# First weight differences on VectorE, the exponential's table behind the last split, and fewer clock-keeping products in a two-layer decoder trunk

## The chip, the core and the metric

The kernel runs on one core of a Trainium2 chip. The metric is the device time of one execution in microseconds; before the change it is 1159.97 us, the median of three runs (1159.62 to 1160.34). The engines are named as in the profile: PE is TensorE (matrix products), PEld its weight loads, DVE is VectorE, ACT is ScalarE, POOL is GpSimd and SP is SyncE, which issues DMAs. Each engine runs its own queue in order, and waits on semaphores of the others.

## The reference

256 tokens of 1024 values pass through two layers. Each layer projects the token matrix once, for three mixers: latent attention with a rotary key, a gated delta rule and a gated recurrence (HGRN2). It merges them by gates and adds a mixture of experts (one of four groups, two of its eight experts).

```
c_q, c_kv, k_rope, qkv, beta, a, ... = split(x @ w_in)          # one combined projection
cos, sin = rope_tables(positions)
o_mla = mla_branch(c_q, c_kv, k_rope, ...)
g = -exp(a_log) * softplus(a + dt_bias)                          # decay of the delta rule
o_dn  = gated_deltanet_branch(qkv, beta, a, ...)
o_hg  = hgrn2(...)
x = LN(alpha*x + mix(o_mla, o_dn, o_hg));  x = LN(alpha*x + moe(x))
```

## The kernel before, in words

The projection needs the normalised tokens with their channels on the partitions. So each layer starts with a norm (`centred` and `norm_scale`: L354 on ScalarE subtracts the mean, L327 to L344 on VectorE work out the scale `rs`, in steps on tiles of 128x2). At L619 VectorE makes two diagonal matrices of `rs`, the tile `sg`. `transposed` multiplies the tokens with them on TensorE (L395, 32 products in two parts, `pm` and `pb`), so that one product turns and scales. ScalarE (L401) and VectorE (L403) evict the results with the norm's gain and bias.

All large products work on split operands: a value is kept as a coarse part and the difference to it, `hTh` and `hTl` for the tokens (L254 on ScalarE, L255 on VectorE, four of each per layer), `wh` and `wl` for weights. `split` makes the latter per piece of 128x1024: a cast on ScalarE (L249) and the difference at L250, on VectorE, or on GpSimd where the piece's name stands in the set `POOLED` (L143). `mm3` then does three products per pair (L261 to L263). The first weights of a layer are those of `cq` (the attention's query rank), in two pieces, `cq.0` and `cq.1`; both names stand in `POOLED`.

Behind `cq` comes `dn_decay`: 24 products with 72 columns (the rotary key and the gates' logits, whose small weights are split at L689 and L691), then a step that loads ScalarE's table with exponential and logarithm (L696), and the decay's own steps (L699 to L752), with the exponential of `a_log` at L719. Then `mla` begins with `ckv` and the sums of squares (L1169 to L1174), and further on `dn_keys` with its first weight `dn_k0`. In layer 0 only, `rope_tables` (L432 to L464) makes sine and cosine from the positions, a chain of VectorE steps on 128x256 tiles with ScalarE's sine (L454, L455) in it; the step at L702 needs them.

What sets the order: a scheduler places each engine's instructions by its own estimates of when operands are ready; `issue_after(x)` keeps what is inside it behind instruction x; SyncE's transfers go in the order of their issue.

The clock-keeping products are `warm(n)`: n products of a constant tile, whose result nobody reads. There are 12 at the start, 8 in layer 0 behind the transposing products (inside `layer`) and 14 between the layers (L1718), in front of the norm.

Of the kernel before, what the change touches and what calls it, by code (L numbers as in the profile page):

```python
# [14 lines left out]
AF = mybir.ActivationFunctionType  # L15
OP = mybir.AluOpType
# [3 lines left out]
DEPTH, D, T = 2, 1024, 256  # L20
# [4 lines left out]
NH = 4  # L25
# [82 lines left out]
class Trunk:  # L108
# [31 lines left out]
        return pool.tile([128, 512], F32, name="ps_" + tag, tag=tag, bufs=self.banks[tag])  # L140


    POOLED = {"cq.0", "cq.1", "gla00.0", "dn_gate1.1"}  # L143
    NBUF, NPRE = 4, 13
    BANKS, MIX_BANKS, MOE_BANKS = {"pa": 1, "pm": 3}, {"po": 1, "pb": 3}, {"sum": 4}
    NB = {"a2": 4, "a4": 7, "d2": 8, "d4": 7, "d8": 1, "wh": 2, "wl": 2, "o4": 4, "sg": 4}
# [94 lines left out]
    def split(self, raw, name):  # L241

        nc = self.nc
        engine = nc.gpsimd if name in self.POOLED else nc.vector
        hi = self.sp.tile([128, 1024], F32R, name="wh", tag="wh", bufs=self.NB["wh"])
# [343 lines left out]
    def layer(self, l):  # L589
        tc, side = self.tc, dict(side="right")  # L590
        with ExitStack() as cl, ExitStack() as cr:
# [7 lines left out]
            with tc.tile_pool(name=f"mix{l}", bufs=1) as mp:  # L599
# [16 lines left out]
                self.hT = [hp.tile([128, KT, T], F32R, name=n, tag=n) for n in ("hTh", "hTl")]  # L616
                diag = self.gp.tile([128, 4, 128], F32, name="sg", tag="sg", bufs=self.NB["sg"])
                for t in range(TB):
                    self.nc.vector.tensor_scalar(diag[:, t], self.ident, self.hrs[:, t], None, op0=OP.mult)  # L619
                self.transposed(self.h, self.hT, self.gb0, tmp=lambda: self.buf("d2", [128, 2, T]), scale=diag)  # L620
                if l == 0:
                    with tc.issue_after(self.latest(self.nc.tensor)):
                        self.warm(8)
                    with tc.issue_after(self.last_lo.ins):
                        self.rope_tables(rope)
                self.router_weights(l)
                self.mix = self.gp.tile([128, TB, D], F32, name="mix")

                self.pq = self.ps("pm")
                self.chunk_cm(self.pq, l, "cq")  # L630
                seq = "dn_decay mla h0 dn_keys dn_inverse dn_queries h1 " \
                      "dn_values hg_forget hg_project hg_local dn_scan hg_scan"
                for n in seq.split():
# [46 lines left out]
    def dn_decay(self, l, mp):  # L680
        nc = self.nc
# [10 lines left out]
        self.done(l, "ba")  # L692
        for k in range(KT):
            self.mm3(ps[0:72, 0:T], [x[:, k] for x in (hi, lo)], [x[:, k] for x in self.hT], k == 0, k == KT - 1)
        with self.tc.issue_after(self.last_sin.ins) if l == 0 else ExitStack():
            self.tc.keep_in_program_order(nc.scalar.preload_act_table_set("natural_log_exp_and_others"))  # L696
        self.small_values(l, self.vrows)
        bc = self.buf("d2", [128, T])
        nc.vector.tensor_copy(bc[64:72], ps[64:72, 0:T])  # L699
# [15 lines left out]
        nc.scalar.activation(x, x, AF.Exp)  # L715
        nc.scalar.activation(x, x, AF.Ln, bias=1.0)
        nc.vector.scalar_tensor_tensor(x, a, 0.0, x, op0=OP.max, op1=OP.add)
        nexp = self.small([128, NH])
        nc.scalar.activation(nexp, self.alog, AF.Exp)  # L719
        nc.vector.scalar_tensor_tensor(g, x, -1.0, nexp[:, None, :].to_broadcast([128, TB, NH]), op0=OP.mult, op1=OP.mult)  # L720
        ps = self.ps()
        gf = g.rearrange("p t h -> p (t h)")
# [791 lines left out]
    def moe(self, l, xp, ep, yc, h1):  # L1514
        nc, A = self.nc, self.A
# [152 lines left out]
        for q in range(nq + 1):  # L1668
# [25 lines left out]
            if 4 <= q < 8:  # L1694
                t, c = divmod(q - 4, 2)
                nc.vector.scalar_tensor_tensor(total[t][c], acc[:, t, 512 * c:512 * c + 512], ALPHA, total[t][c],
                                               op0=OP.mult, op1=OP.add)
# [17 lines left out]
            self.in_turn(self.warm, 10)  # L1715
        self.overflow(l, ep, rv, past, cmb, xc, total, st)
        if l + 1 < DEPTH:
            self.warm(14)  # L1718
            self.centred(acc, total, st)
            self.open_banks(f"mix_banks{l}", self.MIX_BANKS, None)  # L1720
            return
# [9 lines left out]
        i = None  # L1731
        for n in (0, 1, 3, 2):
            t, c, y = pieces[n]
            with self.tc.issue_after(i.ins) if i else ExitStack():
                i = nc.vector.scalar_tensor_tensor(y, y, rs[:, t], rows[1][c], op0=OP.mult, op1=OP.add)  # L1735
            nc.sync.dma_start(self.out[0].rearrange("(t p) d -> p t d", p=128)[:, t, 512 * c:512 * c + 512], y)
            if n == 0:
                with self.tc.issue_after(i.ins):
                    i = nc.vector.scalar_tensor_tensor(pieces[3][2], total[1][1], nm[:, 1], rows[0][1], op0=OP.add, op1=OP.mult)  # L1739
# [35 lines left out]
```

## Time and profile before

| | |
|---|---|
| median of three runs | 1159.97 us |
| profiled execution | 1160.61 us, its span 1158.8 us |
| TensorE busy | 91% of the span |
| VectorE, ScalarE, GpSimd busy | 50%, 37%, 14% |
| mean granted TensorE clock | 0.966 of full speed |

Times within the profile count from the start of the span. Layer 0 starts at 0, the second layer's norm at about 578 us. A row of the timeline gives start and length of one group of like instructions, with the number of them behind x; matrix products are pipelined, so a product's length is longer than the distance to the next, and starts are the better measure. A bracket tells how long the engine was idle before the row and who ended that.

### The profile page before, as it was taken

The page shows a single profiled execution, that of the slowest core. Times are in us where ns is not written, and L with a number is a line of the kernel's source. Part 1 is how long each engine was busy: PE and PEld are TensorE (multiplying, and loading weights), DVE is VectorE, ACT ScalarE, POOL GpSimd, SP SyncE. Part 2 cuts the span into 40 slices and gives each one's busy share as a digit, 9 for nine tenths or more (in the row PEclk, how much of TensorE's full clock was granted, in tenths as well). Part 3 has the DMA queues.
Part 4 walks back from the last instruction along what each step waited for, and adds up shares of the span by engine and source line. Part 5 has one row for each costly group of instructions (what it writes and reads, how often), then busy time and mean ns, then how long its engine had stood idle before and what let it go on. Part 6 is the DMA issues. An engine that isn't in the chain of part 4 may idle for free. (4 is left out here: it accounts for less than half of the span.)

```text
span 1158.8 us, 21407 instructions
## 1 busy us (share of the span) xinstructions
PE 1059.3 (91%) x8896; PEld 775.6 (67%) x8896; DVE 576.9 (50%) x1269; ACT 427.3 (37%) x788; POOL 162.7 (14%) x146
## 2 busy tenths in 40 slices
PE   7999999999999998777889999999999999977775
PEld 5888987777777664434378889777777766543442
DVE  7677754575556422111276876645754562321114
ACT  5764632554445211111067545235444351211111
POOL 2111025101210400000020110450021112000001
PEclk9999999999999999898899999999999999989997
DMA  7632250549965999999983214315599679999994
GB/s 231 200 107 73 91 165 2 169 158 359 424 271 220 410 425 426 426 426 427 366 230 106 74 46 138 110 38 182 196 411 374 251 270 425 426 425 426 427 426 190
DMA packets 104706, 305.58 MB, mean 264 GB/s; under 512 B 20962, under 2 KB 48028, under 8 KB 79516
## 3 DMA queue, kind: packets, MB, share of 16 engines
q1 hardware_dynamic: 104604, 304.15, 68.4%
q8 instruction: 72, 1.18, 0.4%
q14 instruction: 30, 0.25, 0.1%
HBM read 303.08 MB, written 1.05 MB: 262 GB/s over the span
## 5 line engine op out<-in xcount | busy, mean ns | idle before, releaser
L250 DVE TENSOR_TENSOR wl<-w,wh 128x1024 fp32r<-128x1024 f32 x150 | 187.0, 1248 | 161.5 <-ACT wh L249 161.0
L249 ACT CAST wh<-w 128x1024 fp32r<-128x1024 f32 x158 | 165.7, 1049 | 217.7 <-PE ps_po L263 74.7
L1602 PE MATMUL ps_pa<-w,xg 128*32 128x256 f32 x2304 | 175.1, 436 | 59.0 <-DMA w<-in_exp_w_up_dram 29.4
L1602 PEld LDWEIGHTS ps_pa<-w,xg 128*32 128x32 f32 x2304 | 88.0, 125 | 140.4 <-DMA w<-in_exp_w_up_dram 38.2
L1614 DVE SCALAR_TENSOR_TENSOR hm<-ps_pa,ws,hm 128x256 f32<-128x256 f32 x18 | 8.7, 484 | 203.5 <-ACT hm L1613 203.3
L1613 ACT ACTIVATE hm<-ps_pa 128x256 f32<-128x256 f32 x18 | 6.9, 384 | 221.8 <-PE ps_pa L1602 221.8
L261 PE MATMUL ps_pa<-wh,hTh 128*128 128x512 f32 x176 | 71.2, 405 | 2.0 <-ACT hTh L254 0.7
L261 PE MATMUL ps_po<-wh,hTh 128*128 128x512 f32 x176 | 71.2, 405 | 1.9 <-ACT hTh L254 0.7
L262 PE MATMUL ps_po<-wl,hTh 128*128 128x512 f32 x176 | 70.5, 401 | 2.1 <-DVE wl L250 1.6
L262 PE MATMUL ps_pa<-wl,hTh 128*128 128x512 f32 x176 | 70.5, 401 | 2.1 <-DVE wl L250 1.6
L1635 PE MATMUL ps_pm<-w,hmT 128*32 128x512 f32 x576 | 70.8, 595 | 1.3 <-issue 1.3
L263 PE MATMUL ps_pa<-wh,hTl 128*128 128x512 f32 x176 | 70.0, 398 | 0.2 <-DVE hTl L255 0.2
L263 PE MATMUL ps_po<-wh,hTl 128*128 128x512 f32 x176 | 69.9, 397 | 0.2 <-DVE hTl L255 0.2
L1552 PEld LDWEIGHTS ps_pm<-P,h1c 128*128 128x128 f32 x576 | 66.8, 192 | 2.2 <-ACT res L1350 1.0
L1552 PE MATMUL ps_pm<-P,h1c 128*128 128x128 f32 x576 | 67.3, 275 | 0.0
L1561 ACT ACTIVATE xg<-ps_pm,gb 128x128 f32<-128x128 f32 x72 | 32.9, 458 | 71.7 <-DVE xg L1559 71.7
L1574 POOL TENSOR_TENSOR Pw<-P,small 128x128 f32<-128x128 f32 x32 | 12.4, 405 | 306.9 <-PE ps_pm L1581 227.9
L1279 POOL TENSOR_TENSOR mix<-mix,sg 128x512 f32<-128x512 f32 x16 | 28.3, 1792 | 155.4 <-DVE sg L1277 155.4
L1559 DVE TENSOR_SCALAR xg<-ps_pm,gb 128x128 f32<-128x128 f32 x72 | 29.4, 408 | 41.2 <-PE ps_pm L1552 32.2
L263 PE MATMUL ps_po<-hTh,wl 128*128 128x256 f32 (+1 forms) x168 | 48.7, 290 | 0.9 <-DVE wl L250 0.5
L263 PE MATMUL ps_pa<-hTh,wl 128*128 128x256 f32 (+1 forms) x168 | 48.9, 291 | 0.5 <-DVE wl L250 0.5
L261 PE MATMUL ps_pa<-hTh,wh 128*128 128x256 f32 (+1 forms) x168 | 49.2, 293 | 0.0
(442 smaller groups left out, 2134.9 us busy)
## 6 DMA issues: line engine op xcount, KB each, us to landing
w<-in_exp_w_gate_dram SPq DMA_DIRECT2D x66, 1024.0 KB
w<-in_exp_w_up_dram SPq DMA_DIRECT2D x66, 1024.0 KB
w<-in_exp_w_down_dram SPq DMA_DIRECT2D x64, 1024.0 KB
w<-in_w_in_dram SPq DMA_DIRECT2D x58, 1024.0 KB
w<-in_w_out_dram SPq DMA_DIRECT2D x8, 1024.0 KB
w<-in_w_br_a_dram SPq DMA_DIRECT2D x4, 1024.0 KB
w<-in_w_br_b_dram SPq DMA_DIRECT2D x4, 1024.0 KB
w<-in_w_br_c_dram SPq DMA_DIRECT2D x4, 1024.0 KB
```

The costliest lines, as they stand in the source:

```text
L249: nc.scalar.copy(v(hi), raw)
L250: engine.tensor_tensor(v(lo), raw, v(hi).bitcast(F32), op=OP.subtract)
L261: mm(ps, a[0], b[0], start=start, stop=False, skip_group_check=True)
L262: mm(ps, a[0], b[1], start=False, stop=False, skip_group_check=True)
L263: mm(ps, a[1], b[0], start=False, stop=stop, skip_group_check=True)
L1279: nc.gpsimd.tensor_tensor(mv, mv, sg[t], op=OP.add)
L1552: nc.tensor.matmul(ps[:, 128 * k:128 * k + 128], xc[:, t, 4 * h + k], Ps[q][:, t], start=(t == 0), stop=(t == 1))
L1559: nc.vector.tensor_scalar(xg[:, k], o, g, b, op0=OP.mult, op1=OP.add)
L1561: nc.scalar.activation(xg[:, k], o, AF.Identity, scale=g, bias=b)
L1574: self.pool_last = nc.gpsimd.tensor_tensor(e(Pw[:, t]), e(P[:, t]), w, op=OP.mult)
L1602: nc.tensor.matmul(pg[32 * e:32 * e + 32, FF * n:FF * n + FF], xgs[q][k // 4][:, k % 4, 32 * e:32 * e + 32], w[:, FF * k:FF * k + FF], sta ...
L1635: nc.tensor.matmul(ps[c][32 * e:32 * e + 32], hmT[:, i, 32 * e:32 * e + 32], ws[e][:, D * i + 512 * c:D * i + 512 * c + 512], start=(i == ...
```

## The change

It has four edits. The names `cq.0` and `cq.1` leave `POOLED`, so the first two weight differences of both layers are made by VectorE. The products of `cq`, with their splits, are placed behind the second instruction of L619. The 8 clock-keeping products of layer 0 go, and of the 14 between the layers 11 stay. In `dn_decay` the exponential of `a_log` moves up, directly behind the table load, and both are placed behind the last split of the tokens in layer 1 (behind the sine in layer 0, as the table load was).

```
-    POOLED = {"cq.0", "cq.1", "gla00.0", "dn_gate1.1"}
+    POOLED = {"gla00.0", "dn_gate1.1"}
...
                 for t in range(TB):
-                    self.nc.vector.tensor_scalar(diag[:, t], self.ident, self.hrs[:, t], None, op0=OP.mult)
-                self.transposed(self.h, self.hT, self.gb0, tmp=lambda: self.buf("d2", [128, 2, T]), scale=diag)
+                    i = self.nc.vector.tensor_scalar(diag[:, t], self.ident, self.hrs[:, t], None, op0=OP.mult)
+                self.diag = i.ins
+                self.hT_last = self.transposed(self.h, self.hT, self.gb0, tmp=lambda: self.buf("d2", [128, 2, T]), scale=diag)
                 if l == 0:
-                    with tc.issue_after(self.latest(self.nc.tensor)):
-                        self.warm(8)
                     with tc.issue_after(self.last_lo.ins):
                         self.rope_tables(rope)
...
                 self.pq = self.ps("pm")
-                self.chunk_cm(self.pq, l, "cq")
+
+                with tc.issue_after(self.diag):
+                    self.chunk_cm(self.pq, l, "cq")
...
-        with self.tc.issue_after(self.last_sin.ins) if l == 0 else ExitStack():
+        with self.tc.issue_after(self.hT_last if l else self.last_sin.ins):
+            nexp = self.small([128, NH])
             self.tc.keep_in_program_order(nc.scalar.preload_act_table_set("natural_log_exp_and_others"))
+            nc.scalar.activation(nexp, self.alog, AF.Exp)
...
-        nexp = self.small([128, NH])
-        nc.scalar.activation(nexp, self.alog, AF.Exp)
...
         if l + 1 < DEPTH:
-            self.warm(14)
+            self.warm(11)
             self.centred(acc, total, st)
```

Lines of the changed kernel behind L619 are up to three higher (L702 becomes L705, L1173 becomes L1174). The instructions change their order at the two layer starts only, up to the attention's first steps; SyncE's queue keeps its order. On VectorE, at the start of layer 1, before:

```order
L338 SCALAR_TENSOR_TENSOR ln_tmp<-ln_tmp 128x2
L340 TENSOR_SCALAR ln_rs<-ln_tmp,ln_rs 128x1 x2
L342 TENSOR_SCALAR ln_tmp<-ln_rs,ln_v_5356 128x1 x2
L344 TENSOR_SCALAR ln_rs<-ln_tmp,ln_rs 128x1 x2
L619 TENSOR_SCALAR sg<-const,ln_rs 128x128 x2
L403 TENSOR_SCALAR d_5437<-ps_pm,vcol_5038 128x256
L403 TENSOR_SCALAR d_5448<-ps_pm,vcol_5038 128x256 x2
L255 TENSOR_TENSOR hTl<-d_5437,hTh 128x512
L255 TENSOR_TENSOR hTl<-d_5448,hTh 128x512
```

The same place in the changed kernel, where L250 is a weight difference:

```order
L344 TENSOR_SCALAR ln_rs<-ln_tmp,ln_rs 128x1 x2
L619 TENSOR_SCALAR sg<-const,ln_rs 128x128 x2
L250 TENSOR_TENSOR wl<-w,wh 128x1024
L403 TENSOR_SCALAR d_5425<-ps_pm,vcol_5029 128x256
L403 TENSOR_SCALAR d_5436<-ps_pm,vcol_5029 128x256 x2
L255 TENSOR_TENSOR hTl<-d_5425,hTh 128x512
L250 TENSOR_TENSOR wl<-w,wh 128x1024
L255 TENSOR_TENSOR hTl<-d_5436,hTh 128x512
L255 TENSOR_TENSOR hTl<-d_5446,hTh 128x512
L403 TENSOR_SCALAR d_5456<-ps_pb,vcol_5029 128x256 x2
```

The two weight differences came into VectorE's queue, one between the diagonal and the first eviction, the other between the first and the second hTl; layer 0 has the same order.

On ScalarE, in layer 0 behind the token splits, before (L249 is a weight cast, L454 and L455 the sine, L1169 and L1170 the attention's squares):

```order
L689 CAST wh<-w 128x8x8
L249 CAST wh<-w 128x1024
L454 ACT_TABLE_LOAD
L454 ACTIVATE d_146<-d_146 128x256
L455 ACTIVATE d_146<-d_146 128x256
L696 ACT_TABLE_LOAD
L719 ACTIVATE small<-alog 128x4
L1169 ACTIVATE a_468<-ps_pm 128x512
L249 CAST wh<-w 128x1024
```

In the changed kernel:

```order
L690 CAST wh<-w 128x8x8
L249 CAST wh<-w 128x1024
L1170 ACTIVATE a_459<-ps_pm 128x512
L249 CAST wh<-w 128x1024
L454 ACT_TABLE_LOAD
L454 ACTIVATE d_146<-d_146 128x256
L455 ACTIVATE d_146<-d_146 128x256
L698 ACT_TABLE_LOAD
L699 ACTIVATE small<-alog 128x4
L531 ACTIVATE lb_e<-lb_e 128x8
L1171 ACTIVATE a_459<-ps_pm 128x256
```

A square and a weight cast went ahead of the sine and its table; the second square (L1171) stands behind both table loads.

On TensorE, in layer 0 within and behind the ckv products (L261 to L263 into `ps_pm`), before:

```order
L261 MATMUL ps_pm<-hTh,wh 128x256
L262 MATMUL ps_pm<-hTl,wh 128x256
L702 MATMUL ps_pb<-d_396,mconst 128x256
L707 MATMUL ps_pb<-const,d_396 128x8 x2
L263 MATMUL ps_pm<-hTh,wl 128x256
```

In the changed kernel (`ps_po` takes dn_k0):

```order
L263 MATMUL ps_pm<-hTh,wl 128x256
L1174 MATMUL ps_pm<-a_459,ones 128x256 x2
L261 MATMUL ps_po<-hTh,wh 128x256
L262 MATMUL ps_po<-hTl,wh 128x256
L263 MATMUL ps_po<-hTh,wl 128x256
L1175 MATMUL ps_pm<-a_459,ones 128x256
L705 MATMUL ps_pb<-d_388,mconst 128x256
L710 MATMUL ps_pb<-const,d_388 128x8 x2
```

The step that needs the rope tables (L702, now L705) stood ten products before the end of ckv, and stands behind ckv, the sums of squares and three products of dn_k0 now.

## Rows read from the trace of the kernel before

**Rows 1.** The page: busy times (share of span, instructions), and one costly group.
```profile
PE 1059.3 (91%) x8896; PEld 775.6 (67%) x8896; DVE 576.9 (50%) x1269; ACT 427.3 (37%) x788; POOL 162.7 (14%) x146
...
L250 DVE TENSOR_TENSOR wl<-w,wh 128x1024 fp32r<-128x1024 f32 x150 | 187.0, 1248 | 161.5 <-ACT wh L249 161.0
```
**Rows 2.** Timeline of VectorE, layer 1: start, length, group [idle before <-releaser].
```profile
579.02 0.45 DVE L337 TENSOR_SCALAR ln_tmp<-ln_rs,ln_v 128x1 f32<-128x1 f32 x2
579.50 2.34 DVE L338 SCALAR_TENSOR_TENSOR ln_tmp<-ln_tmp 128x2 f32<-128x2 f32 x1
...
583.10 2.07 DVE L619 TENSOR_SCALAR sg<-const,ln_rs 128x128 f32<-128x128 f32 x2 [0.26 <-DMA mconst<-in_consts_dram]
```
**Rows 3.** Timeline of GpSimd, layer 1.
```profile
579.47 2.35 POOL L250 TENSOR_TENSOR wl<-w,wh 128x1024 fp32r<-128x1024 f32 x1
582.54 2.34 POOL L250 TENSOR_TENSOR wl<-w,wh 128x1024 fp32r<-128x1024 f32 x1 [0.72 <-ACT wh L249]
```
**Rows 4.** Timeline of VectorE, layer 0.
```profile
7.98 0.46 DVE L337 TENSOR_SCALAR ln_tmp<-ln_rs,ln_v 128x1 f32<-128x1 f32 x2
8.47 0.16 DVE L338 SCALAR_TENSOR_TENSOR ln_tmp<-ln_tmp 128x2 f32<-128x2 f32 x1
...
9.54 0.47 DVE L619 TENSOR_SCALAR sg<-const,ln_rs 128x128 f32<-128x128 f32 x2
...
13.26 3.56 DVE L255 TENSOR_TENSOR hTl<-d,hTh 128x512 fp32r<-128x512 f32 x2
...
17.65 1.46 DVE L255 TENSOR_TENSOR hTl<-d,hTh 128x512 fp32r<-128x512 f32 x2
```
**Rows 5.** Timeline of GpSimd, layer 0.
```profile
11.14 5.13 POOL L250 TENSOR_TENSOR wl<-w,wh 128x1024 fp32r<-128x1024 f32 x2 [9.35 <-ACT wh L249]
```
**Rows 6.** Timeline of TensorE, layer 1.
```profile
578.98 3.18 PE L365 MATMUL ps_pa<-bits 128*128 128x512 bf16 x14 [0.30 <-DVE ln_rs L334]
585.17 3.03 PE L395 MATMUL ps_pm<-sg,res 128*128 128x128 f32 x16 [3.02 <-issue]
588.00 2.61 PE L395 MATMUL ps_pb<-sg,res 128*128 128x128 f32 x16
590.37 0.36 PE L261 MATMUL ps_pm<-hTh,wh 128*128 128x256 f32 x1
```
**Rows 7.** Timeline of TensorE, layer 0.
```profile
10.36 1.95 PE L395 MATMUL ps_pm<-sg,res 128*128 128x128 f32 x16
12.14 1.95 PE L395 MATMUL ps_pb<-sg,res 128*128 128x128 f32 x16
13.93 1.89 PE L365 MATMUL ps_pa<-bits 128*128 128x512 bf16 x8
...
22.73 0.34 PE L263 MATMUL ps_po<-hTh,wl 128*72 128x256 f32 x1 [0.45 <-DVE wl L691]
...
28.83 0.67 PE L702 MATMUL ps_pb<-d,mconst 64*128 64x256 f32 x2 [1.49 <-DVE lb_e L530]
...
29.65 0.58 PE L263 MATMUL ps_pm<-hTh,wl 128*128 128x256 f32 x1
...
33.15 0.47 PE L261 MATMUL ps_pa<-hTh,wh 128*128 128x256 f32 x1
```
**Rows 8.** Timeline of ScalarE, layer 0: the two table loads.
```profile
23.09 1.28 ACT L454 ACT_TABLE_LOAD   x1
...
25.23 1.28 ACT L696 ACT_TABLE_LOAD   x1
```
**Rows 9.** Timeline of ScalarE, layer 1: the load that goes.
```profile
586.47 1.28 ACT L719 ACT_TABLE_LOAD   x1
```
**Rows 10.** Windows: stretch, its length, each engine's busy time, granted clock, DMA share, GB/s.
```profile
27.00:30.00 3.00, 1.51 (x8) 0.98 (x8) 2.89 (x11) 1.73 (x4) 0.00 (x0) 0.93 0.59 125
30.00:33.00 3.00, 3.00 (x13) 2.82 (x13) 1.02 (x11) 0.97 (x2) 0.00 (x0) 0.50 0.93 223
...
585.00:588.00 3.00, 2.83 (x17) 2.86 (x17) 0.70 (x2) 2.08 (x4) 0.00 (x0) 0.66 0.67 142
```

## The prediction

> **What bounds the kernel now.** I read the page first, for the engine that has least slack [rows 1]: TensorE is busy 91% of the span, VectorE 50%, GpSimd 14%. The waits by releaser agree: outside the expert stage TensorE seldom waits, so what a mixer stage can give is the places where TensorE stands still or runs at its lower clock. The timeline of both layer starts shows where. In layer 1, TensorE does clock-keeping products until 582.16 and begins the transposing products of L395 at 585.17, after 3.02 us of idleness [rows 6]. What it waits for is the diagonal that L619 makes from the norm's scale, and on VectorE two steps of that norm are far longer than their work [rows 2]: L338, a 128x2 step, takes 2.34 us, and the pair of L619 takes 2.07. GpSimd, meanwhile, works at the two first weight differences, 579.47 to 581.82 and 582.54 to 584.88 [rows 3]. L338 ends at 581.84, and the L619 pair at 585.17: each of the two ends with or just behind a GpSimd difference. In layer 0, where GpSimd is idle at that point, the same two lines take 0.16 and 0.47 us [rows 4]. There the collision comes later: the first pair of L255 takes 3.56 us beside the GpSimd differences (11.14 to 16.27), and the second pair, after them, 1.46 [rows 4, 5]. So I read the first weight differences on GpSimd as what holds VectorE up at both layer starts.
>
> The granted clock tells the second part [rows 10]: it is at its upper level (2.4 GHz) until about 29.6 in layer 0, then 0.50 (1.2 GHz) from 30 to 33, behind a stop of 1.5 us ended by L702 at 28.83 [rows 7]; and 0.66 on average from 585 to 588, behind the 3.02 us of idleness.
>
> **The differences move to VectorE: layer 1.** VectorE does such a difference in 1.25 us [rows 1], GpSimd in 2.35. L619's start then follows the norm chain of layer 0, where L337 begins at 7.98 and the L619 pair ends at 10.01, 2.03 us later [rows 4]. From L337 at 579.02 [rows 2] that is 581.05, some 581.3 with the chain's few extra queue steps. The clock-keeping products, 11 now instead of 14, take 3.18 x 11/14 = 2.50 us from 578.98 and end at 581.5 [rows 6]. TensorE begins L395 at about 581.6 instead of 585.17: 3.6 us. With next to no idleness before it I take the clock as held: the 32 products of L395, which take from 585.17 to 590.37, 5.2 us [rows 6], then take what they do in layer 0, from 10.36 to about 14.1, 3.75 us [rows 7]: 1.45 us. Against that stands the new work on VectorE. The first difference lies between L619 and the first eviction, about 581.3 to 582.5, while TensorE makes the products that this eviction takes, so it is free. The second lies behind the first hTl (L255), and the next hTl stands behind it: I take a stop of 0.6 us in the cq products, and 0.25 for the later ones. Its bounds are nothing (the cover holds) and 1.25 (all of it is seen). Layer 1: 3.6 + 1.45 - 0.85 - 0.1 (the 72-wide products start closer behind their own difference) = 4.1 us.
>
> **Layer 0, the same edit and the removed clock-keeping products.** VectorE's 2.1 us stall in L255 goes, and 2 x 1.25 us of differences come, the first in the idle time before the first eviction. The 8 clock-keeping products (13.93 to 15.82) [rows 7] kept TensorE busy until the first hTl and wl; now cq starts at about 14.1 and stops about 1.1 us for its second hTl, which stands behind the second difference. By that walk cq ends 0.8 us earlier. The two small differences for the 72-wide products are now issued among the first steps of the rope tables, not behind most of them, so the wait before L263 at 22.73 [rows 7] goes: 0.6 us (0.72 from the product in front, less 0.12 for a product).
>
> **The order behind it.** Before, TensorE's queue has L702 in the middle of the ckv products; L702 needs the rope tables, and so ScalarE's sine, which has a table load in front and one behind (1.28 us each, 23.09 and 25.23) [rows 8]. That is the 1.5 us stop. In the new order ckv's products, the first sums of squares and three products of dn_k0 stand ahead of L705 (the same line as L702 before). The stop goes (1.6 us with the uneven starts around it), and with it, if the clock holds, the stretch at 1.2 GHz: from 29.65 to 33.15 it takes 3.50 us [rows 7], of which some 2.9 at granted clock 0.50, so 1.45 us. In its place comes another stop. The sum of squares at L1175 waits for ScalarE, which does that square only behind sine, cosine and both table loads: by the walk TensorE stands from 27.8 to 28.9, 1.1 us. (Its bounds: nothing, and the 2.14 us from load to load [rows 8].) Three dn_k0 products and the L702 work change places and add 0.3 at most; I take it. Layer 0: 0.8 + 0.6 + 1.6 + 1.45 - 1.1 + 0.3 = 3.65 us, about 3.7.
>
> The new stop hangs on what a table switch costs. The rows show 1.28 us for each load, and from load to load 2.14, in which two activations of 0.4 us fit, so nothing else is paid for [rows 8]. The Trainium skill, page "ScalarE: Activation LUTs", section "What ACT_TABLE_LOAD costs", counts a drain of about 1.38 us on top. If that were paid here, two switches would lengthen the stop by 2 x 1.38 = 2.8 us, an estimate from that page, and the whole would be near 1155; the rows speak against it.
>
> **The exponential and its table.** In layer 1 this removes one table load at 586.47 [rows 9], which stands between the first eviction and the first hTh on ScalarE. That hTh moves ahead by 1.3 us at most, but TensorE is at L395 then, so the gain is in the 3.6 + 1.45 already and I count nothing more. In layer 0 it only sets the place of load and exponential behind the sine; without it, its cover is the same ScalarE queue. No DMA issue moves: the order on SyncE's queue is the same before and after, and the streams it issues in this stretch are consumed later by more than the shift. The GpSimd queue only loses work.
>
> **The sum.** 4.1 + 3.7 = 7.8 us. The mixer stages are bound by TensorE, and the start of the expert stream hangs on the position of the mixer's end, so I carry both through to the end at full size. The profiled execution took 1160.61 (span 1158.8), 0.64 over the median of 1159.97; I subtract from the median: **1152.2 us** (a span near 1151).
>
> **Rivals.**
> (a) The clock falls in layer 0. Nothing now fills the 1.1 us stop at 14.9 and the 1.1 us one at 27.8. The rows have a wait of about 0.6 (22.73) with the clock held after it, and one of 1.5 (28.83) with a fall after it [rows 7, 10]; 1.1 lies between. A fall costs the 1.45 us worked out above: 1153.7 for one, 1155.1 for two. The Trainium skill, page "TensorE: Matmul & The Clock Gate", Part 1, says that "the default state is throttled, and activity releases the throttle"; the fall behind 28.83 agrees, and by that rule any stop puts the clock at stake, these two as well.
> (b) L619 in layer 1 is held by a transfer. Its row names DMA mconst as what ended the 0.26 us before it [rows 2]. Were that the real bound, L619 could not begin before 583.1, 2.1 us later than the chain allows, and the time is 1154.3, with idleness that lowers the clock 1155.6. Against it: 0.26 us is what five queue steps take, and the wait ends with nothing else late.
> (c) VectorE becomes the bound in layer 0: the two differences push back every hTl and the rope tables behind them, and ScalarE's sine with them, by their 2.5 us, and the 3.7 of layer 0 shrinks to 1.2: 1154.7.
> (d) Slower. The long L338, L619 and L255 come from something else than GpSimd. Then the norm chain of layer 1 still ends at 585.2, with 0.7 us more idleness, as 3 clock-keeping products are gone; VectorE has two differences more in front of hTl, 0.85 us seen in layer 1 and 2.5 in layer 0, with no stall given back: 1160.0 + 3.3 = 1163.3. It decides from the point where less than these 3.3 us of the stalls come back; the excess of L338 and L619 in layer 1 alone is 2.18 + 1.6 = 3.8. Against it speak both coincidences of ends and the 0.16 us of the same step in layer 0 [rows 2 to 5].
> (e) The shift of the mixer is absorbed by the expert stream, whose transfers run at full rate: then next to nothing is seen. The start of that stream hangs on buffers that the mixer frees, so I give it little.
>
> **Chances.** Forecast 1152.2 with its stops between their bounds (1150.3 to 1153.2): 0.55. (a) 0.22, (b) 0.06, (c) 0.09, (d) 0.04, (e) 0.04. The range 1150.4 to 1154.6 takes in the forecast, one fall of the clock and most of (b); what lies outside is the second fall, part of (c), (d) and (e). A measurement of this kernel tells about 0.2% (2.3 us) from no change: faster means below 1157.65. Faster 0.92, same 0.04, slower 0.04.
>
> **What would show it.** In the new trace: L338 of layer 1 at 0.2 us or less and the L619 pair ended by 581.5; the first L395 at 581.6 with the granted clock at 1.00 from 580 to 600; cq's last product near 592.1; in layer 0 no stop inside the ckv products, one of about 1 us near 28 ended by ScalarE's square, clock 1.00 from 24 to 36, and the attention products of L1231 about 4 us earlier. The prediction is wrong if L338 stays long, if the clock falls between 14 and 36, if L619 begins at 583 again, or if the shift at 600 us (4.1 + 3.7) isn't found at the end of the span.

## The result, and the profile after

The changed kernel takes 1152.9 us (median of 8 runs, 1151.9 to 1157.0), beside 1159.5 us for the kernel before in the same comparison (8 runs): a ratio of 0.9948, with a 95% interval of 0.9936 to 0.9960. That is 6.6 us, or 4.6 to 7.4 by the interval. The forecast was 1152.2 us and 7.8 us; the time lies in its range, and the gain is smaller than forecast by about 1.2 us, the forecast gain lying just above that interval. Measured once more (e12 below), the changed kernel takes 1154.9 us beside 1159.1; the fourteen runs together have a median of 1153.2 us.

The timeline of VectorE at the start of layer 1 in the changed kernel (start, length, group, idle time before and what ended it; line 619 and those before keep their numbers):

```profile
576.53 0.45 DVE L337 TENSOR_SCALAR ln_tmp<-ln_rs,ln_v 128x1 f32<-128x1 f32 x2
577.02 0.16 DVE L338 SCALAR_TENSOR_TENSOR ln_tmp<-ln_tmp 128x2 f32<-128x2 f32 x1
...
578.43 0.68 DVE L619 TENSOR_SCALAR sg<-const,ln_rs 128x128 f32<-128x128 f32 x2 [0.26 <-DVE ln_rs L344]
579.02 1.22 DVE L250 TENSOR_TENSOR wl<-w,wh 128x1024 fp32r<-128x1024 f32 x1
580.20 0.54 DVE L403 TENSOR_SCALAR d<-ps_pm,vcol 128x256 f32<-128x256 f32 x1
```

L338 takes 0.16 us where it took 2.34, and the pair of L619 0.68 where it took 2.07 [rows 2]. From L337 to the end of the L619 pair it is now 2.6 us, before 6.1. L619 begins when its own norm steps are done. TensorE in the same place:

```profile
576.37 2.53 PE L365 MATMUL ps_pa<-bits 128*128 128x512 bf16 x11 [0.30 <-DVE ln_v L333]
579.02 2.03 PE L395 MATMUL ps_pm<-sg,res 128*128 128x128 f32 x16
580.89 1.95 PE L395 MATMUL ps_pb<-sg,res 128*128 128x128 f32 x16
```

There is next to no idle time left between the clock-keeping products and L395 (they end at 578.90), and the two parts take 2.03 and 1.95 us instead of 3.03 and 2.61 [rows 6]. TensorE in layer 0:

```profile
6.41 4.51 PE L365 MATMUL ps_po<-bits 128*128 128x512 bf16 x12
10.76 1.95 PE L395 MATMUL ps_pm<-sg,res 128*128 128x128 f32 x16
...
29.20 0.70 PE L1175 MATMUL ps_pm<-a,ones 128*128 128x256 f32 x2 [0.74 <-ACT a L1171]
29.83 0.70 PE L705 MATMUL ps_pb<-d,mconst 64*128 64x256 f32 x2
...
46.90 0.83 PE L1247 MATMUL ps_pm<-const,a 128*128 128x128 f32 x4 [1.27 <-DVE a L1244]
```

The stop of 1.5 us in front of the rope step [rows 7] is gone; the new one in front of L1175 is 0.74 us. The last row matters below: the attention's transposes at L1247 wait 1.27 us, where the same products (L1246) waited 0.91 before:

```profile
49.67 0.82 PE L1246 MATMUL ps_pm<-const,a 128*128 128x128 f32 x4 [0.91 <-DVE a L1243]
```

Windows of the changed kernel (stretch, length, busy times of TensorE, its loads, VectorE, ScalarE, GpSimd, then the granted clock, DMA share, GB/s):

```profile
27.00:30.00 3.00, 2.26 (x13) 1.62 (x12) 2.83 (x12) 2.97 (x6) 0.00 (x0) 1.00 0.61 127
30.00:33.00 3.00, 3.00 (x23) 2.65 (x24) 2.78 (x16) 2.23 (x8) 0.00 (x0) 1.00 0.87 179
...
582.00:585.00 3.00, 2.31 (x20) 2.12 (x19) 3.00 (x6) 2.16 (x4) 0.00 (x0) 1.00 0.63 134
585.00:588.00 3.00, 3.00 (x26) 2.89 (x26) 2.86 (x11) 1.90 (x4) 0.00 (x0) 1.00 0.65 138
```

In this execution the clock stays at its upper level where it fell to 0.50 and 0.66 before [rows 10].

**How the gain adds up along the span.** Starts of the same VectorE step in the two profiled executions, compared, tell how far ahead a kernel is at each place. The changed kernel is ahead by 2.8 us from the attention of layer 0 on (L1241 before at 55.55, its counterpart at 52.78), by 2.6 at the norm of layer 1 (L327, 578.02 and 575.42), and by 6.8 from 613 us up to the last norm in front of the experts (926.26 and 919.49). The expert stream then moves the difference by a microsecond either way in single executions; 1158.8 - 1151.1 = 7.7 us is what this pair of spans shows. So the change gives 2.8 us in layer 0, of which 2.6 are left at the norm of layer 1, and 4.2 in layer 1.

The same reading for all kernels, each against the profiled execution of the kernel before. "Layer 0" is the lead at 300 us, "layer 1" what the lead grows by from the norm at 578 to 640 us. The last column is the length of the twelve clock-keeping products at the very start, which all kernels share:

| kernel | median us | layer 0 | layer 1 | first 12 products, us |
|---|---|---|---|---|
| before | 1159.5 | 0 | 0 | 4.05 |
| changed | 1152.9 | 2.8 | 4.2 | 4.51 |
| changed, once more (e12) | 1154.9 | 2.9 | 4.2 | 4.16 |
| GpSimd's differences back (e1) | 1164.9 | 0.0 | 0.7, then -5.1 | 5.30 |
| VectorE edit alone (e2) | 1155.4 | 0.1 | 4.0 | 5.27 |
| GpSimd reads beside (e6) | 1162.0 | -1.5 | 0.5 | 4.37 |
| GpSimd writes beside (e7) | 1154.0 | 2.6 | 3.6 | 4.60 |
| no placement behind L619 (e3) | 1154.6 | 2.3 | 3.8 | 4.71 |
| clock-keeping back (e4) | 1155.8 | -0.1 | 3.3 | 5.30 |
| table and exponential back (e5) | 1157.2 | -3.0 | 3.9 | late start |
| no products between layers (e8) | 1156.1 | 0.1 | 3.1 | 5.30 |
| wait at L1247 filled (e9) | 1153.2 | 1.6 | 4.2 | 5.30 |
| second difference later (e10) | 1153.7 | -1.1 | 4.9 | 5.29 |
| both (e11) | 1153.7 | 2.1 | 4.9 | 4.29 |

Two things limit the table. Its leads are those of one profiled execution each, which is not always a typical one: it is the slowest of its kernel's runs in e4, e8 and e10 (1157.1, 1157.4 and 1156.3 us), and the fastest in e6 and e11 (1159.2 and 1152.0). And the lead in layer 0 contains the start: with 5.3 us for the twelve products, L395 begins at 11.6 to 11.7, against 10.36 before and 10.76 in the changed kernel. For e1 the lead at 617 us is 0.8, so 0.7 is taken there. The medians of the later kernels stand beside kernels before of 1159.1 (e1, e2, e6, e7, e9 to e12) and 1159.8 us (e3, e4, e5, e8).

### The profile page after: what moved, and what is told of

It reads as the page before. It is cut to its first block, busy times and chain, and to the rows that moved or that the text cites. A ratio compares the mean times of both kernels' runs of the same rounds, so it can differ in the third digit from the quotient of the medians.

```text
span 1151.1 us, 21384 instructions
## 1 busy us (share of the span) xinstructions
PE 1051.9 (91%) x8885; PEld 770.4 (67%) x8885; DVE 574.9 (50%) x1273; ACT 425.5 (37%) x787; POOL 153.7 (13%) x142
## 5 line engine op out<-in xcount | busy, mean ns | idle before, releaser
L250 DVE TENSOR_TENSOR wl<-w,wh 128x1024 fp32r<-128x1024 f32 x154 | 191.5, 1245 | 160.7 <-ACT wh L249 156.1
L249 ACT CAST wh<-w 128x1024 fp32r<-128x1024 f32 x158 | 165.7, 1049 | 216.9 <-PE ps_po L263 74.7
L1603 PE MATMUL ps_pa<-w,xg 128*32 128x256 f32 x2304 | 172.0, 428 | 60.9 <-DMA w<-in_exp_w_up_dram 32.5
L261 PE MATMUL ps_pa<-wh,hTh 128*128 128x512 f32 x176 | 71.3, 405 | 2.0 <-ACT hTh L254 0.7
L261 PE MATMUL ps_po<-wh,hTh 128*128 128x512 f32 x176 | 71.2, 405 | 2.0 <-ACT hTh L254 0.8
L263 PE MATMUL ps_po<-wh,hTl 128*128 128x512 f32 x176 | 70.0, 398 | 0.2 <-DVE hTl L255 0.2
L263 PE MATMUL ps_pa<-wh,hTl 128*128 128x512 f32 x176 | 69.9, 397 | 0.2 <-DVE hTl L255 0.2
L261 PE MATMUL ps_po<-hTh,wh 128*128 128x256 f32 (+1 forms) x168 | 49.2, 293 | 0.0
L263 PE MATMUL ps_po<-hTh,wl 128*128 128x256 f32 (+1 forms) x168 | 48.7, 290 | 0.5 <-DVE wl L250 0.5
L263 PE MATMUL ps_pa<-hTh,wl 128*128 128x256 f32 (+1 forms) x168 | 48.7, 290 | 0.5 <-DVE wl L250 0.5
```

The costliest lines, as they stand in the source:

```text
L249: nc.scalar.copy(v(hi), raw)
L250: engine.tensor_tensor(v(lo), raw, v(hi).bitcast(F32), op=OP.subtract)
L261: mm(ps, a[0], b[0], start=start, stop=False, skip_group_check=True)
L263: mm(ps, a[1], b[0], start=False, stop=stop, skip_group_check=True)
L1603: nc.tensor.matmul(pg[32 * e:32 * e + 32, FF * n:FF * n + FF], xgs[q][k // 4][:, k % 4, 32 * e:32 * e + 32], w[:, FF * k:FF * k + FF], sta ...
```

## The experiments

**GpSimd's differences back.** One edit of the changed kernel undone:

```
-    POOLED = {"gla00.0", "dn_gate1.1"}
+    POOLED = {"cq.0", "cq.1", "gla00.0", "dn_gate1.1"}
```

> The changed kernel with one edit undone: cq.0 and cq.1 are made on GpSimd again, everything else (order behind the diagonal, fewer clock-keeping products, table) stays. Theory (GpSimd's differences hold VectorE up): L338 of layer 1 is 2 us long again and the layer-1 gain of 4.0 us goes; layer 0 loses 1 to 3 us too; 1157 to 1160 us in all. Rival (the other three edits bring the gain): L338 stays at 0.16 us and the time stays within 1.5 us of 1152.9.

It takes 1164.9 us (5 runs; 1.0050 of before, 1.0037 to 1.0063), slower than the kernel before. In layer 1 L338 is long again, beside GpSimd's first difference; the L619 pair is not (0.48 us), as the second difference begins only at 585.74. VectorE, then GpSimd:

```profile
579.53 2.17 DVE L338 SCALAR_TENSOR_TENSOR ln_tmp<-ln_tmp 128x2 f32<-128x2 f32 x1
```

```profile
579.34 2.35 POOL L250 TENSOR_TENSOR wl<-w,wh 128x1024 fp32r<-128x1024 f32 x1
```

L338 ends at 581.70, 0.02 us behind GpSimd's step at 581.68, and TensorE waits 2.03 us for L395. Of the layer-1 gain 0.7 us are left behind cq. But that is not where most of the time goes. The expected 1157 to 1160 was missed because the planner put the rest of layer 1 in another order. Its waits on TensorE from 600 to 730 us (line waited for, total, times, longest):

```profile
PE ps_pb L854 <- DVE small L308: 2.7, 1, 2.7
PE ps_pa L263 <- DVE wl L250: 1.7, 1, 1.7
```

And windows there:

```profile
645.00:650.00 5.00, 4.01 (x38) 2.98 (x38) 4.15 (x13) 0.00 (x0) 0.49 (x1) 0.72 0.00 0
...
695.00:700.00 5.00, 5.00 (x32) 5.00 (x32) 3.65 (x8) 1.69 (x2) 0.00 (x0) 0.66 0.20 37
```

The first wait is 0.8 us in the kernel before and in the changed one, the second 0.5. Each is followed by a stretch at a lower granted clock. From 617 to 926 us this costs 5.9 us, and the two differences of cq lie 50 us and more ahead of it. So this run shows the mechanism in layer 1, but its total is not the price of the edit.

**The VectorE edit alone.** The kernel before, with only this:

```
-    POOLED = {"cq.0", "cq.1", "gla00.0", "dn_gate1.1"}
+    POOLED = {"gla00.0", "dn_gate1.1"}
```

> The kernel before with only the one edit: cq.0 and cq.1 on VectorE. Theory: most of the gain comes from this alone. In layer 1 the first difference now stands inside the norm chain on VectorE, which costs 1.2 us of the 4.0, and the table load in front of the first hTh stays; so 2.5 to 3 us in layer 1 and 0 to 2.5 in layer 0: 1154 to 1157 us. Rival (the order behind the diagonal is what counts): under 1.5 us of gain, 1158 or more.

1155.4 us (6 runs; 0.9965, 0.9953 to 0.9977), within the expected range, but for another reason in part. Layer 1 gains 4.0 us, not 2.5 to 3. The first difference does stand in the norm chain:

```profile
577.82 0.46 DVE L337 TENSOR_SCALAR ln_tmp<-ln_rs,ln_v 128x1 f32<-128x1 f32 x2
578.20 1.21 DVE L250 TENSOR_TENSOR wl<-w,wh 128x1024 fp32r<-128x1024 f32 x1
579.33 0.15 DVE L338 SCALAR_TENSOR_TENSOR ln_tmp<-ln_tmp 128x2 f32<-128x2 f32 x1
...
581.19 1.23 DVE L250 TENSOR_TENSOR wl<-w,wh 128x1024 fp32r<-128x1024 f32 x1
582.33 0.54 DVE L403 TENSOR_SCALAR d<-ps_pm,vcol 128x256 f32<-128x256 f32 x1
```

It delays L338 by 1.13 us. But then both differences are made in front of the first eviction, and the stop inside cq doesn't occur: the new work shows once, as 1.13 us in the chain here or as the 0.69 us stop in cq in the changed kernel. In layer 0 this kernel is 1.5 us ahead at 49 us, though its L395 began 1.3 us later than before, and only 0.1 at 53: the clock falls (0.66 from 48 to 52), behind a wait of 1.63 us in front of L1246.

**Does GpSimd do it, and with what?** Both kernels add work on GpSimd to the changed kernel, for cq.0 and cq.1, that nobody waits for.

```
+            spare = self.sp.tile([128, 1024], F32, name="spare", tag="spare", bufs=1)
+            nc.gpsimd.tensor_tensor(v(spare), raw, v(hi).bitcast(F32), op=OP.subtract)
```

> The changed kernel, and beside it GpSimd works out the same two differences once more into a spare tile that nobody reads (both layers). Nothing waits for this work. Theory (GpSimd's two-input step blocks VectorE while it runs): L338 in layer 1 ends with the GpSimd step, about 2 us longer, and VectorE's own differences and L255 are stretched where they meet the second one; loss of 3 to 5 us over both layers, 1156 to 1158 us. Rival (something else held L338): time and L338 as in the changed kernel, 1152.9 us and 0.16 us.

1162.0 us (10 runs; 1.0024, 1.0015 to 1.0033). Layer 1 keeps 0.5 us of its 4.2, and layer 0 goes from 2.8 ahead to 1.5 behind. In layer 0 TensorE, VectorE and ScalarE do their instructions in the changed kernel's order. The loss is 9 us by the medians and 8 by the two leads, more than the 3 to 5 expected (the profiled execution, 1159.2 us, is the fastest of the ten). In this kernel the code lies three lines lower (L338 is L341). VectorE, in layer 1 and in layer 0:

```profile
579.75 2.34 DVE L341 SCALAR_TENSOR_TENSOR ln_tmp<-ln_tmp 128x2 f32<-128x2 f32 x1
...
13.67 1.36 DVE L258 TENSOR_TENSOR hTl<-d,hTh 128x512 fp32r<-128x512 f32 x1
14.96 3.38 DVE L250 TENSOR_TENSOR wl<-w,wh 128x1024 fp32r<-128x1024 f32 x1
```

GpSimd, in layer 1 and in layer 0:

```profile
579.72 2.36 POOL L253 TENSOR_TENSOR spare<-w,wh 128x1024 f32<-128x1024 f32 x1
...
11.14 6.11 POOL L253 TENSOR_TENSOR spare<-w,wh 128x1024 f32<-128x1024 f32 x2 [9.35 <-ACT wh L249]
```

L341 ends at 582.09, GpSimd's step at 582.08. In layer 0 a difference on VectorE takes 3.38 us instead of 1.22. GpSimd's work stands there in one row of 6.11 us for two steps, longer than 2 x 2.35 = 4.7: each engine waits for the other in turn. TensorE then stands for the second hTl (L258), and the clock is 0.52 from 20 to 23, behind this wait:

```profile
18.99 0.39 PE L265 MATMUL ps_pm<-hTl,wh 128*128 128x256 f32 x1 [2.93 <-DVE hTl L258]
```

With nothing changed but this added work, the long L338 is GpSimd's doing.

The other kernel fills the spare tile instead:

```
+            for _ in range(2):
+                nc.gpsimd.memset(spare, 0.0)
```

> The changed kernel, and beside it GpSimd fills a spare tile of 128x1024 four times per layer (about 0.95 us each), work that reads nothing and that nobody waits for. If any GpSimd work blocks VectorE: a loss like that of the kernel with the GpSimd differences, 2 to 4 us where fills meet L338 or L619. If it is the reading that collides: L338 at 0.16 us, L619 at 0.5 to 0.7 us, and the time stays at 1152.9 us.

1154.0 us (4 runs; 0.9953, 0.9938 to 0.9967). Here L338 is L342 and L619 is L623. VectorE, and then GpSimd:

```profile
577.22 0.16 DVE L342 SCALAR_TENSOR_TENSOR ln_tmp<-ln_tmp 128x2 f32<-128x2 f32 x1
578.62 1.27 DVE L623 TENSOR_SCALAR sg<-const,ln_rs 128x128 f32<-128x128 f32 x2 [0.26 <-DVE ln_rs L348]
579.22 1.22 DVE L250 TENSOR_TENSOR wl<-w,wh 128x1024 fp32r<-128x1024 f32 x1
```

```profile
576.73 0.95 POOL L254 MEMSET spare<- 128x1024 f32 x1
577.63 0.29 POOL L478 CAST ones<-d 128x128 fp32r<-128x128 f32 x1
577.86 2.97 POOL L254 MEMSET spare<- 128x1024 f32 x3
```

The two-input steps, L342 and the difference, run at their normal 0.16 and 1.22 us in the middle of fills. The pair of L623, with one tile as input, takes 1.27 instead of 0.68 us, and layer 1 keeps 3.6 of 4.2 us. So neither expectation is right as a whole: reading is what holds the two-input steps, and a one-input step can be held by a fill as well. It is the second step of the pair: it takes 0.88 us and ends at 579.90, 0.08 behind the end of a fill, where the first takes 0.29. The one-input steps on 128x1 beside the same fills (L346, L348) were not held: 0.45 and 0.33 us a pair, as in the changed kernel (0.46 and 0.33). The Trainium skill, page "SBUF — State Buffer", section "SBUF: two separate sides", has a rule of this form: the two engines share a port pair as an exclusive lock, which a VectorE step with two inputs from on-chip memory (SBUF) contends for only against GpSimd work that reads, and one in a fast two-port mode against any. The rows agree, 0.16 us against 2.34 for the same step; that L623 runs in such a mode no row shows.

**The order behind the diagonal.**

```
-                with tc.issue_after(self.diag):
+                with ExitStack():
                     self.chunk_cm(self.pq, l, "cq")
```

> The changed kernel without the placement behind the diagonal. In layer 1 the first difference then stands in front of L338 in VectorE's queue, the second cast comes earlier, and a third table load comes back in front of the small weights. Theory of the prediction (the difference in the norm chain costs its 1.2 us): layer-1 gain 2.7 instead of 4.0 us, 1154.2 us. Rival, from the kernel with VectorE alone (its layer 1 gained 4.0 us too, with the difference inside the chain): what is lost in the chain comes back in the cq products, whose stop goes; layer-1 gain 3.8 to 4.2 us and 1152.9 us. Layer 0 is unchanged in either case.

1154.6 us (5 runs; 0.9956, 0.9939 to 0.9973), layer 1 3.8 us. The placement is worth 0.4 us of lead, against the 1.3 that the prediction's reasoning gave and near the rival's nothing; the medians don't resolve it.

**The clock-keeping products.** All 11 that were removed are back:

```
-            self.warm(11)
+            self.warm(14)
...
+                    with tc.issue_after(self.latest(self.nc.tensor)):
+                        self.warm(8)
```

> The changed kernel with the 8 clock-keeping products of layer 0 and 14 between the layers back. Theory: in layer 1, 14 products end at 579.6 on the changed kernel's time axis, 0.6 us behind the diagonal, and cost 0.5 us; in layer 0 the 8 stand in front of the first cq product and the planner puts the later work in another order, so the layer-0 gain of 2.8 us falls to 1.5, or to nothing if the clock falls near 48 us. 1154.5 to 1157 us. Rival (they were needed for the clock): the time falls below 1152.

1155.8 us (5 runs; 0.9961, 0.9945 to 0.9976). Layer 1 loses 0.9 us, about the three products (0.7 us). Layer 0 loses all its lead: 0.9 us with the slow start, and the rest behind a changed order, with a stop of 1.2 us in front of the rope step (at 30.3) and a clock of 0.50 from 33 to 36.

**The table and the exponential** where they were before:

```
-        with self.tc.issue_after(self.hT_last if l else self.last_sin.ins):
-            nexp = self.small([128, NH])
+        with self.tc.issue_after(self.last_sin.ins) if l == 0 else ExitStack():
...
-            nc.scalar.activation(nexp, self.alog, AF.Exp)
...
+        nexp = self.small([128, NH])
+        nc.scalar.activation(nexp, self.alog, AF.Exp)
```

> The changed kernel with the exponential of a_log and its table where they were before. Theory: worth nothing on the path in layer 1 (layer-1 gain 3.8 to 4.1 us); in layer 0 the order around L1175 changes, so the 0.7 us stop there moves; 1152 to 1154 us. Rival (the table load between the first eviction and the first hTh was part of the gain): layer-1 gain 2.7 us, 1154.2 us.

1157.2 us (10 runs; 0.9980, 0.9967 to 0.9994): both expectations missed. Layer 1 is nearly untouched (3.9 us), as the theory says. The loss is in layer 0, where ScalarE's queue now has the eviction of dn_k0 (L774) ahead of the attention's exponentials (L1240); TensorE's row follows:

```profile
46.86 0.58 ACT L774 COPY sg<-ps_po 128x512 f32<-128x512 f32 x1 [0.22 <-PE ps_po L263]
47.34 0.40 ACT L1240 ACTIVATE a<-a,mla_st 128x128 f32<-128x128 f32 x1
```

```profile
49.67 0.82 PE L1247 MATMUL ps_pm<-const,a 128*128 128x128 f32 x4 [2.85 <-DVE a L1244]
```

The eviction waits for the end of dn_k0, the exponentials for the eviction, and TensorE stands 2.85 us in front of L1247 instead of 1.27. The clock then falls. (This execution also began its first products 1 us late, for a transfer, and they took 5.30 us, so L395 began 1.8 us later than in the changed kernel; that part is not the edit's.)

**No clock-keeping between the layers.**

```
-            self.warm(11)
             self.centred(acc, total, st)
```

> The changed kernel without the 11 clock-keeping products between the layers; TensorE then stands still from 576.1 to 579.0. Theory (idleness of about 3 us lowers the clock, as in front of L395 in the kernel before): L395 and the first cq products run at 1.2 GHz, granted clock 0.6 to 0.7 from 579 to 583, and the layer-1 gain falls by 1.2 to 1.5 us: 1154.3 us. Rival (ten products in front hold the clock): same as the changed kernel, 1152.9 us.

1156.1 us (6 runs; 0.9966, 0.9954 to 0.9979). In layer 1 it is as the theory says, 2.86 us of idleness, a granted clock of 0.51 from 582 to 585, and 1.1 us of lead lost. But layer 0 is the same instruction for instruction as in the changed kernel, and it lost 2.6 us there. One part is the start: the twelve products, which begin at half speed in every execution, took 5.30 us instead of 4.51. The other part is here, on TensorE and in the windows:

```profile
47.92 0.82 PE L1247 MATMUL ps_pm<-const,a 128*128 128x128 f32 x4 [1.27 <-DVE a L1244]
```

```profile
48.00:51.00 3.00, 2.82 (x16) 1.89 (x17) 2.53 (x6) 3.00 (x5) 0.00 (x0) 0.76 0.47 167
51.00:54.00 3.00, 3.00 (x16) 2.73 (x15) 1.74 (x8) 1.14 (x5) 0.00 (x0) 0.67 0.00 0
```

It is the same wait of 1.27 us in front of L1247 as in the changed kernel, and this time the clock falls behind it. The lead shrinks from 1.9 us at 43 to 0.15 at 66. All six runs take 1155.4 us or more. With 1.1 us lost in layer 1, and a fall in layer 0 that comes and goes, some should lie near 1154; so why the clock fell there is open.

**The wait filled, the second difference later, and both.** Five clock-keeping products ahead of the transposes of layer 0 (e9); the second difference behind the second hTl (e10):

```
+                if l == 0 and g == 0 and t == 0:
+                    for _ in range(5):
+                        nc.tensor.matmul(ps, self.bits[:, 0], self.bits[:, 0:1].to_broadcast([128, 4, 128]), start=True, stop=True)
...
+        with self.tc.issue_after(self.los[1]) if name == "cq.1" else ExitStack():
             engine.tensor_tensor(v(lo), raw, v(hi).bitcast(F32), op=OP.subtract)
```

> The changed kernel with 5 clock-keeping products in layer 0 shortly in front of the transposes that wait 1.27 us near 47 us. They take 1.08 us of TensorE's time there and push other products into the wait, so the position behind it stays. Theory (that wait is where the clock falls in some executions, at a price of 1.6 us, and isn't in others): the wait shrinks to 0.2 us, the granted clock is 1.00 from 45 to 57 in the profile, and every run lies near the best of the changed kernel: median 1152.0 to 1152.8 us, spread under 2 us. Rival (the spread comes from elsewhere, the expert stream for one): median 1153 to 1154, spread of 4 us as before, or 1 us slower through the added products.

1153.2 us (5 runs, 1152.9 to 1155.3; 0.9949, 0.9936 to 0.9962). The profiled execution had a slow start (5.30 us), like that of e8, and the wait is 0.20 us, on TensorE and then the windows:

```profile
6.58 5.30 PE L365 MATMUL ps_po<-bits 128*128 128x512 bf16 x12
...
48.05 0.92 PE L1250 MATMUL ps_pm<-const,a 128*128 128x128 f32 x4 [0.20 <-DVE a L1244]
```

```profile
48.00:51.00 3.00, 2.51 (x18) 1.90 (x19) 2.69 (x7) 2.98 (x6) 0.00 (x0) 1.00 0.20 70
51.00:54.00 3.00, 3.00 (x26) 2.98 (x24) 2.91 (x8) 1.51 (x6) 0.00 (x0) 1.00 0.00 0
```

The clock holds, and layer 0 keeps 1.6 us of lead where e8 kept 0.1. The median is above the expected range and the spread of 2.5 us above the expected 2. The trace agrees with the theory of the fall, but it is one execution, and the changed kernel and e12 held the clock with the wait unfilled; that the fall is all of the spread is not borne out.

> The changed kernel with the second weight difference behind the second hTl on VectorE, in both layers. Theory: the cq stops of 0.76 us (layer 0) and 0.69 us (layer 1) go, since the second difference isn't needed before the 25th cq product; 1.0 to 1.4 us faster, 1151.5 to 1152 us; the clock near 48 us falls in some runs as before. Rival (VectorE is the bound there, whatever the order): the stop moves to the second half of cq and nothing is gained, 1152.9 us or more.

1153.7 us (5 runs; 0.9947, 0.9934 to 0.9960). Layer 1 gains 0.7 us, as expected: the stop in cq is gone there. Layer 0 has new stops instead (1.08 us in front of the sums of squares), and in this execution the clock falls behind that one.

> Both of the last two edits on the changed kernel: 5 clock-keeping products ahead of the transposes, and the second difference behind the second hTl. If both theories hold, 1150.7 to 1151.6 us with a spread under 2 us. If the order edit gains nothing, 1152 to 1153; if the products cost more than they keep, 1152 or more with the spread of the changed kernel.

1153.7 us (5 runs, 1152.0 to 1154.9; 0.9953, 0.9940 to 0.9966). The same 0.7 us in layer 1, and 0.6 less than the changed kernel in layer 0. No version is shown to beat the changed kernel. One that moves the second difference in layer 1 only wasn't tried.

> The changed kernel once more, nothing altered, for its spread beside the three others. If the clock falls by chance at the wait near 47 us, its times again lie in two groups, 1152 to 1153 and 1154.5 to 1157 us, and the profile shows either 1.00 throughout or about 0.7 from 48 to 54. If the first group was the rule and the rest disturbance, at least four of five lie below 1153.5 us.

1154.9 us (6 runs; 0.9960, 0.9945 to 0.9975): 1152.2, 1152.7 and 1153.4 against 1156.4, 1156.4 and 1156.5. With the eight runs of the first comparison that makes nine of fourteen between 1151.9 and 1153.8 us, and five between 1155.4 and 1157.0. So there are two groups, 3 to 4 us apart. Both profiled executions belong to the lower one and show 1.00 from 45 to 57 us. The record also has the mean granted clock of every run: 0.965 to 0.968 in the five, 0.968 to 0.974 in the nine. So a lower clock goes with the longer time; in which place isn't seen. The kernel's own two medians are 2 us apart, and those of e2, e3, e4, e7, e9, e10 and e11 (1153.2 to 1155.8) don't tell them from it: what these experiments show stands in their traces.

## Why the prediction was right, and where it was not

**The cause was right.** GpSimd's differences held VectorE up: e6 brings the long L338 back by added work alone, and e2 has 4.0 of layer 1's 4.2 us with that one edit. For layer 0 no such share is shown: in e1, e2, e4 and e5 its lead at 300 us is 0.1 or less, in executions that also began L395 at least 0.8 us later than the changed kernel's and in which the clock fell.

**Layer 1 was right in sum and in its terms.** Forecast 4.1 us, measured 4.2 and 4.2. L338 took 0.16 us; the first L395 began 6.2 us earlier on the span's axis, of which 2.6 are layer 0's, so 3.6 as forecast; the 32 products went at the upper clock, in 3.6 us from start to start (579.02 to 582.60) instead of 5.2. The stop for the second hTl in cq was 0.69 us (0.6 taken), and no later one came, for which 0.25 were taken. It is smaller than its upper bound, and e10 shows that it could be had back.

**The term that was mis-sized is layer 0:** 3.7 us forecast, 2.8 and 2.9 measured. The mechanism held: the wait in front of the 72-wide products went, the 1.5 us stop and its half-speed stretch went, and one new stop came in front of L1175. Three things separate the sizes.

- The start took 0.4 us longer than in the execution of before (L395 at 10.76 against 10.36), which is the start's chance and not the change: in e12 the same twelve products took 4.16 us. There, with 0.3 us of it back, the lead was larger by 0.15.
- Without the start, the changed kernel is ahead by 3.6 us at the seventh product of dn_k0 (31.13 against 34.29), close to the 3.65 of the sum, but by terms that cancel, which is luck. The way to the end of the 72-wide products gave 1.7 us, not 0.8 + 0.6. The half-speed stretch gave 1.7, not 1.45: [rows 10] have 0.50 for all of 30 to 33 us and 0.93 before, which is more than the 2.9 us taken. The new stop was 0.9 us from start to start (0.74 idle), not 1.1. Against these, the "0.3 at most" for products that change places was wrong in its sign: they cost 0.5 us. Most of it is the pair of L1175, which takes 0.63 us to the next start behind its stop, where the pair of L1174 took 0.24 before.
- The wait in front of L1247 grew from 0.91 to 1.27 us: TensorE's last product ahead of it comes 3.1 us earlier than before (45.36 against 48.49), VectorE's softmax steps only 2.8. That step was not in the walk, which ended at L1231. One of the signs named, the attention products of L1231 "about 4 us earlier", wasn't met: they came 2.4 us earlier (42.54 against 44.98).

**The range.** 1152.9 us lies in it; the second median, 1154.9, lies 0.3 us above its end. The prediction's upper end for the forecast alone, 1153.2, is worked out wrongly: with both stops at their upper bounds the sum gives 1153.6.

**Rival (a) was right as a mechanism and wrong in its place.** The stops at 14.9 and 27.8 measured 0.76 and 0.74 us, and the clock held behind them in both profiled executions of the changed kernel and in e8, whose layer 0 is the same. It fell at L1247, in e8, at 1.6 us (1.45 forecast for a fall). With the slower start this makes 2.6 of the 3 to 4 us between the two groups. That the upper group is this case is not shown: no profile of it was taken.

**The others.** (b) L619 began at 578.43 with its own chain; the transfer named in its row before was no bound. (c) In layer 0 VectorE's rope steps came 1.7 us later (L453 at 25.88 against 24.16) and ScalarE's sine 2.0 (26.53 against 24.49), but TensorE saw no more of it than the 0.74 us in front of L1175. (d) fell with L338. (e) fell for the changed kernel: the 6.8 us are there at 926 us, and 6.6 in the median. But part of a shift can be taken up in the experts of layer 0: e9 is 1.6 us ahead at 300 us and 2.6 at 578, as far as the changed kernel, and e10 goes from -1.1 to -0.1. The full 1.28 us per table load, without a drain, held: the loads in the changed kernel are 2.03 us apart (25.24 and 27.27) with two activations between. The sentence that the exponential's move hides behind the same queue in layer 0 was wrong: e5's median is 4 us above that of the changed kernel's fourteen runs, and its trace shows a place in ScalarE's queue 20 us later as what ends TensorE's longest wait there.

## What to carry to other kernels

Two engines that look independent can exclude each other; a tiny step that lasts as long as a large one elsewhere, and ends with it, is the sign. Take the larger step to the engine that would have waited anyway, and look for the gap in which it is free. And where a planner sets the order, one undone edit is not one changed thing: compare leads place by place along the span before a total is put down to it.

## What the runs showed of the hardware that was not expected

- The same wait of 1.27 us, in the same instructions, is followed by the upper clock in six executions (changed, e12, e3, e6, e7, e10) and by 0.76 and 0.67 in another (e8).
- The twelve products at the very start run at half speed for a part that differs from execution to execution: 4.05 to 5.30 us for the same work. Where they took 5.27 us or more, the clock fell again between 30 and 55 us in five of six executions (e1, e2, e4, e8, e10), all but the one whose wait was filled (e9); in the six between 4.16 and 4.71 us it never fell there (in e6 it fell earlier, behind its 2.93 us wait). The late start of e5 is left out of this count; it took 5.30 us too, and the clock fell from 50 us on. The kernel before, at 4.05 us, fell behind its 1.5 us stop. That is a coincidence seen over kernels of different order, not a cause that was tested.
- A VectorE step with two inputs isn't touched by a GpSimd fill (0.16 us), and is held to the last by a GpSimd step that reads (2.34 us).
